# Second weight parts a turn later, six raw buffers, one factor multiply moved and full-row second key parts in a two-layer attention and conv-FFN trunk

## The chip, the cores and the metric

The kernel runs on one core of a Trainium2 chip. The metric is the device time of one execution in microseconds (us); smaller is better. A core has five engines that work side by side, each through its own list of instructions in order: TensorE (PE, matrix products), VectorE (DVE), ScalarE (ACT), GpSimd (POOL) and SyncE (SP, which here issues most DMAs). They wait for each other through semaphores. SBUF is the core's memory with 128 partitions, PSUM the banks into which PE writes.

## What is computed

Two layers over 256 positions of width 1024, in float32. Layer 0 mixes tokens with dilated attention A (three groups of 16 heads of 64, one window and dilation each, merged by their softmax denominators), layer 1 with block attention B. Each layer ends in a gated FFN with a causal convolution of width 3.

```python
for i in range(DEPTH):                       # 2 layers
    hn = rmsnorm(x, attn_norm[i])
    x = x + (mixer_dilated if i % 2 == 0 else mixer_moba)(hn, w_qkv, q_gain, k_gain, w_o, cos, sin)
    hn = rmsnorm(x, ffn_norm[i])
    x = x + conv_ffn(hn, ffn_w_up[i], ffn_conv_w[i], ffn_conv_b[i], ffn_w_down[i])

def mixer_dilated(h, w_qkv, q_gain, k_gain, w_o, cos, sin):
    qkv = (h @ w_qkv).reshape(B, S, 3, N_DIL, N_HEADS, HEAD_DIM)
    q = apply_partial_rope(rmsnorm(qkv[:, :, 0], q_gain[:, None, :]), cos, sin)
    k = apply_partial_rope(rmsnorm(qkv[:, :, 1], k_gain[:, None, :]), cos, sin)
    v = qkv[:, :, 2]
    # per group: scores, mask, softmax, times v; then the groups weighted by denominators
    return attn @ w_o

def conv_ffn(h, w_up, conv_w, conv_b, w_down):
    u = h @ w_up
    uc = conv_b + sum(conv_w[j] * up[:, j:j + S] for j in range(CONV_WIDTH))
    gate, val = uc[..., :D_FF], uc[..., D_FF:]
    return (jax.nn.silu(gate) * val) @ w_down
```

## The kernel before

**Products in two parts.** A float32 product is made of products of rounded numbers: a matrix is split into a first part (`whi` of a weight, a rounded copy) and a second part (`wlo`, the rest), and `mm3` adds three products of 128x512: activations' first part by `whi` (L380), their second part by `whi` (L381), their first part by `wlo` (L382).

**The weight stream.** `Stream` cuts all weights into 244 parts of 128x1024 in the order of use. `load` starts the DMA of a raw part on SP (4 raw buffers, `RAW`); `start` makes `whi` from it on ACT (L85); `finish` makes `wlo` on DVE (L94) and calls `load` again, so the load of a raw part stands behind the `wlo` of the part four before it. `take` hands parts to the products, `release` frees their `whi` and `wlo` (8 of each, `WB`).

**Turns.** All work around the products is placed by `turn`, once for each piece of a product. A turn runs, in this order: `ws.start`, the tasks in the table `first`, one `ws.finish`, the tasks in `pre`, the rest of `ws.finish`, the products themselves (with the tasks in `mid` in them), the tasks in `post`. `at(table, n, task)` puts a task into a table n turns later. Each engine then runs its instructions in the order in which they were written.

**Attention.** For each section of 4 heads, `qk_block` makes q and k. When a block's product is done, ACT copies it (`sq`, `qk`); a turn later `head_sums` runs on DVE (L432 to L444), and POOL makes the factors `rs_y` from it (L257, L259); another turn later `factors` multiplies (L453, DVE); PE transposes (L469), ACT makes the first parts of keys and queries (L505), and `second_parts` makes the rest on DVE (L511, L513). `step_A` makes scores for two heads. For group 0 of attention A the head's own half of the partitions of `qT` and `kT` holds first parts and the other half second or copied first parts, so that L575 contracts all 128 rows; the product with the second parts of the keys, `kL`, contracts the head's 64 rows (L577), for two heads side by side. L590 makes the scores of the other groups from 64x64 pieces. `step_E` takes the masked scores and their maximum on DVE (L603) and the exponentials on ACT (L613); `step_R` scales by the denominator on DVE (L620, L623); `step_T` transposes on PE (L630); `step_V` copies to SBUF (ACT) and `step_C` multiplies by v (L657).

The order within a turn:

```python
        ws.start(min(pump, 1 if len(ws.parts) - ws.taken >= AHEAD else 2))
        for f, a in first.pop(t, ()):
            f(*a)
        ws.finish(1)
        for f, a in pre.pop(t, ()):
            f(*a)
        ws.finish()
```

Of the kernel before, what the change touches and what calls it, by code (L numbers as in the profile page):

```python
# [11 lines left out]
F32R = mybir.dt.float32r  # L12
# [5 lines left out]
P = 128  # L18
# [11 lines left out]
NSEC = NH // HS  # L30
NEG = -1.0e30
PAIRS = ((128, 1), (512, 4), (2048, 16))
RAW, WB, QB, TB, AHEAD = 4, 8, 5, 6, 5

FINE, WARM = 4, 9

PUMPS = (0, 0, 1, 2, 1, 1, 1, 0, 2, 1, 1)

# [8 lines left out]
def r32(ap):  # L47
    return ap.bitcast(F32)


class Stream:
# [33 lines left out]
                    self.nc.scalar.activation(hi[:, i], raw[:, i], AF.Copy)  # L85
                self.parts.append((hi, lo))

    def finish(self, n=WB):

        while self.done < len(self.parts) and n > 0:  # L90
            n -= 1
            hi, lo = self.parts[self.done]
            for i in self.pieces(self.done):
                self.nc.vector.tensor_sub(lo[:, i], self.raw[self.done][:, i], r32(hi[:, i]))  # L94
            self.done += 1
            self.load()
# [5 lines left out]
    def take(self, n):  # L102
        while len(self.parts) < self.taken + n:
            k = len(self.parts)
            self.pump()
            assert len(self.parts) > k
        self.taken += n
        return [(i, *self.parts[i]) for i in range(self.taken - n, self.taken)]

    def release(self, *units):  # L110
# [7 lines left out]
def trunk_kernel(ctx, tc, x, a_w_qkv, a_w_o, b_w_qkv, b_w_o, ffn_norm, ffn_w_up, ffn_w_down, gains, pack, mask_a, mask_b,  # L118
# [61 lines left out]

    def turn(fn, pump=2):
        t = now[0]
        ws.start(min(pump, 1 if len(ws.parts) - ws.taken >= AHEAD else 2))
        for f, a in first.pop(t, ()):
            f(*a)
        ws.finish(1)
        for f, a in pre.pop(t, ()):
            f(*a)
        ws.finish()
        if fn is not None:  # L190
            fn()
        for f, a in post.pop(t, ()):
            f(*a)
        now[0] += 1
# [190 lines left out]
    def attention(xT, norms, ng, g0, mask):  # L385
# [3 lines left out]
        moff = 3 * P if dil else P  # L389
        aT = new_T()  # L390

        def product(done):

            box = {}

            def part(c, u):
                def go():
                    if c == 0:
                        box[u] = ws.take(2)
                    if u == 0:  # L400
                        box["acc", c] = new_acc()
                    for i, (_, hi, lo) in enumerate(box[u]):
                        if i == 1:
                            for f, a in mid.pop(now[0], ()):
                                f(*a)
                        for kk in range(2):
                            k = (u + i) * 2 + kk
                            mm3(box["acc", c], xT, k, c, hi[:, kk].rearrange("p j n -> p (j n)"),
                                lo[:, kk].rearrange("p j n -> p (j n)"), k == 0, k == 7)
                    if c == 1:  # L410
                        ws.release(*box[u])
                    if u == 2:
                        done(c, box["acc", c])
                return go

            for c in range(2):
                for u in (0, 2):
                    yield part(c, u)

        def qk_block(g, res, rq):  # L420
            res.append(None)

            def done(c, acc):
# [6 lines left out]
            def head_sums(c, qk, sq):  # L430
                ssq = sp.tile([P, 8], F32, name="qssq", bufs=2)
                nc.vector.tensor_reduce(ssq, sq.rearrange("p (h d) -> p h d", d=HD), axis=AX.X, op=ALU.add)  # L432
                rs = rsqrt_pool(ssq, 1.0 / HD, norms[c].eps)

                t4 = qk.rearrange("p (j h d) -> p j h d", j=2, d=HD)
                ra = sp.tile([P, 2, HS, 16], F32, name="ra", bufs=1)
                rb = sp.tile([P, 2, HS, 16], F32, name="rb", bufs=1)
                cg = CG[:, c, g0 + g]
                sg = SG[:, c, g0 + g]
                nc.vector.tensor_mul(ra, t4[:, :, :, 0:16], cg[:, :, None, :].to_broadcast([P, 2, HS, 16]))  # L440
                for lo_, hi_ in ((0, 8), (8, 0)):
                    nc.vector.tensor_mul(rb[:, :, :, lo_:lo_ + 8], t4[:, :, :, hi_:hi_ + 8],
                                         sg[:, :, None, lo_:lo_ + 8].to_broadcast([P, 2, HS, 8]))
                nc.vector.tensor_add(t4[:, :, :, 0:16], ra, rb)  # L444
                at(first, 1, factors, c, qk, rs)

            def factors(c, qk, rs):

# [7 lines left out]
            def transpose(c, qk):  # L456
                if c == 0:
                    if dil and g > 0:
                        res[g] = [bp.tile([P, 2, 2, P], F32R, name="t0", bufs=TB) for _ in range(2)]
                    elif dil:  # L460
                        res[g] = [*(bp.tile([P, 2, 2, S], F32R, name="kT", bufs=QB) for _ in range(2)),
                                  bp.tile([P, 2, S], F32R, name="kL", bufs=2)]
                    else:
                        res[g] = (bp.tile([P, 2, 2, P], F32R, name="t0", bufs=TB),
                                  bp.tile([P, 2, 2, P], F32R, name="t0", bufs=TB),
                                  bp.tile([P, 2, 2, S], F32R, name="kT", bufs=QB))
# [18 lines left out]
                if dil and g > 0:  # L485
                    plain(res[g][c])
                elif dil:

                    qT, kT, kL = res[g]
                    for e in range(2):  # L490
                        r, o = slice(e * HD, e * HD + HD), slice(HD - e * HD, P - e * HD)
                        copies.append((kT[r, e, :, cs], k[r], gk[r]))
                        copies.append((qT[r, e, :, cs], q[r], 1.0))
                        subs.append((kT[r, e, :, cs], kL[r, :, cs], k[r], gk[r]))
                        subs.append((qT[r, e, :, cs], qT[o, e, :, cs], q[r], None))
                        at(post, 4 + e, nc.gpsimd.tensor_copy, kT[o, e, :, cs], kT[r, e, :, cs])
                else:
                    t0, q1, kT = res[g]
                    split(kT[:, :, 0, cs], kT[:, :, 1, cs], k, gk)
                    if c == 0:  # L500
                        plain(t0)
                    else:
                        split(q1[:, 0], q1[:, 1], q, None)
# [54 lines left out]
        def step_A(sec, c, heads, qkT, v, rq):  # L558
# [5 lines left out]
            for i in range(0, len(heads), 2):  # L564
# [7 lines left out]
                if dil:  # L572
                    qT, kT, kL = qkT[0]
                    for e, (s2, o, rows, pr) in enumerate(two):
                        nc.tensor.matmul(s2[:, o:o + S], qT[:, e, pr, cs], kT[:, e, pr], start=True, stop=False)  # L575
                    for e, (s2, o, rows, pr) in enumerate(two):
                        nc.tensor.matmul(s2[:, o:o + S], qT[rows, e, pr, cs], kL[rows, pr], start=False, stop=True)  # L577
                else:
                    for a, b in ((0, 0), (1, 0), (0, 1)):
                        for s2, o, rows, pr in two:  # L580
# [89 lines left out]
        for sec in range(NSEC):  # L670
            qk, v, rq = [], vs[sec], {}
            for s, c, heads in last if sec == NSEC - 1 else odd if sec % 2 else plan:
                at(post, s, step_A, sec, c, heads, qk, v, rq)
            gens = [qk_block(g, qk, rq) for g in range(ng)] + ([v_first(v)] if dil else [])
            gens += [v_last(vs[sec // 2 * 2:sec // 2 * 2 + 2])] if sec in V_TURN[ng] else []
            fns = [fn for gen in gens for fn in gen]
            if sec == 0:
# [326 lines left out]
```

## Time and profile before

| what | value |
|---|---|
| median of 3 runs | 798.54 us (798.48 to 799.37) |
| profiled execution: device time | 798.97 us |
| profiled execution: span in the trace | 797.1 us |
| PE busy in the span | 779.1 us, 98% |
| DVE busy | 565.8 us, 71% |
| ACT busy | 487.1 us, 61% |
| POOL busy | 101.3 us, 13% |
| PE's mean granted clock, share of full speed | 0.997 |

The times in the rows below count from the start of the span. By the trace the kernel goes through a start (to about 49 us), the rest of attention A (to 283), its output product (to 304), the first conv-FFN (to 480), attention B (to 590), its output product (to 620) and the second conv-FFN (to 797). A bracket at the end of a row of a timeline is the engine's idle time just before it and what ended it. Ends of matmuls are modelled, so how fast PE goes is read from start to start.

### The profile page before, as it was taken

The page shows a single profiled execution, that of the slowest core. Times are in us where ns is not written, and L with a number is a line of the kernel's source. Part 1 is how long each engine was busy: PE and PEld are TensorE (multiplying, and loading weights), DVE is VectorE, ACT ScalarE, POOL GpSimd, SP SyncE. Part 2 cuts the span into 40 slices and gives each one's busy share as a digit, 9 for nine tenths or more (in the row PEclk, how much of TensorE's full clock was granted, in tenths as well). Part 3 has the DMA queues.
Part 4 walks back from the last instruction along what each step waited for, and adds up shares of the span by engine and source line. Part 5 has one row for each costly group of instructions (what it writes and reads, how often), then busy time and mean ns, then how long its engine had stood idle before and what let it go on. Part 6 is the DMA issues. An engine that isn't in the chain of part 4 may idle for free.

```text
span 797.1 us, 13374 instructions
## 1 busy us (share of the span) xinstructions
PE 779.1 (98%) x5010; PEld 672.5 (84%) x5010; DVE 565.8 (71%) x1026; ACT 487.1 (61%) x827; POOL 101.3 (13%) x133
## 2 busy tenths in 40 slices
PE   8999999999999999999999999999999999999997
PEld 6778878888878779999999988777778999999996
DVE  6885776885686656788667676777757687767762
ACT  7668676676775636556554655867755565555550
POOL 3540241340134000000000002132100000000000
PEclk9999999999999999999999999999999999999999
DMA  8676545445446425566655462743426457655631
GB/s 261 192 236 192 149 128 185 133 153 165 132 138 230 137 80 167 175 212 210 216 186 185 159 206 91 232 133 107 160 79 192 152 175 247 213 159 176 204 124 53
DMA packets 107920, 133.90 MB, mean 168 GB/s; under 512 B 5968, under 2 KB 92368, under 8 KB 107856
## 3 DMA queue, kind: packets, MB, share of 16 engines
q1 hardware_dynamic: 107280, 130.96, 52.3%
q0 software_dynamic: 576, 2.10, 0.7%
q8 instruction: 39, 0.64, 0.4%
q14 instruction: 25, 0.20, 0.1%
HBM read 131.99 MB, written 1.05 MB: 167 GB/s over the span
## 4 chain that ended last, share of the span: by engine, by line
PE 79%; DVE 9%; ACT 4%; POOL 3%; issue 2%; DMA 2%; SPq 0%; DVEq 0%; ACTq 0%; POOLq 0%
PE acc L770 10%; PE acc L769 10%; PE acc L768 10%; PE acc L380 9%; PE acc L382 8%; PE acc L381 8%; DVE wlo L94 3%; PE S L809 3%; PE S L810 3%; PE S L811 3%; PE PT L811 2%; PE PT L809 2%; PE PT L810 2%; PE O L657 2%; PE PT L630 2%
## 5 line engine op out<-in xcount | busy, mean ns | idle before, releaser
L94 DVE TENSOR_TENSOR wlo<-raw,whi 128x1024 fp32r<-128x1024 f32 (+1 forms) x248 | 291.7, 1209 | 80.1 <-ACT whi L85 79.1
L85 ACT ACTIVATE whi<-raw 128x1024 fp32r<-128x1024 f32 (+1 forms) x248 | 249.1, 1039 | 20.6 <-PE PT L810 10.8
L380 PE MATMUL acc<-whi,xT 128*128 128x512 f32 x448 | 183.6, 410 | 2.3 <-ACT whi L85 1.6
L770 PE MATMUL acc<-xT,wlo 128*128 128x256 f32 x640 | 181.1, 283 | 0.0
L768 PE MATMUL acc<-xT,whi 128*128 128x256 f32 x640 | 181.1, 283 | 0.0
L769 PE MATMUL acc<-xT,whi 128*128 128x256 f32 x640 | 181.1, 283 | 0.0
L382 PE MATMUL acc<-wlo,xT 128*128 128x512 f32 x448 | 176.6, 394 | 2.9 <-DVE wlo L94 2.8
L381 PE MATMUL acc<-whi,xT 128*128 128x512 f32 x448 | 175.8, 392 | 0.4 <-DVE xT L369 0.2
L769 PEld LDWEIGHTS acc<-xT,whi 128*128 128x128 f32 x640 | 122.7, 192 | 1.3
L768 PEld LDWEIGHTS acc<-xT,whi 128*128 128x128 f32 x640 | 122.7, 192 | 1.3
L770 PEld LDWEIGHTS acc<-xT,wlo 128*128 128x128 f32 x640 | 122.7, 192 | 0.0
L382 PEld LDWEIGHTS acc<-wlo,xT 128*128 128x128 f32 x448 | 84.4, 188 | 24.0 <-DVE wlo L94 5.4
L380 PEld LDWEIGHTS acc<-whi,xT 128*128 128x128 f32 x448 | 84.5, 189 | 21.9 <-issue 2.6
L381 PEld LDWEIGHTS acc<-whi,xT 128*128 128x128 f32 x448 | 84.7, 189 | 16.9 <-DVE xT L369 1.5
L785 DVE SCALAR_TENSOR_TENSOR qk<-acc,pk,qk 128x255 f32<-128x255 f32 (+1 forms) x160 | 65.9, 473 | 21.4 <-ACT qk L782 21.2
L782 ACT ACTIVATE qk<-acc,pk 128x256 f32<-128x256 f32 x80 | 40.6, 557 | 28.1 <-PE acc L770 28.1
L259 POOL TENSOR_TENSOR rs_y<-rs_v,mhalf 128x8 f32<-128x8 f32 x32 | 53.6, 1674 | 2.7
L794 ACT ACTIVATE kT<-qk 128x512 fp32r<-128x512 f32 x22 | 13.9, 632 | 56.9 <-DVE qk L792 56.9
L257 POOL TENSOR_SCALAR rs_v<-qssq,rn_e 128x8 f32<-128x8 f32 x32 | 14.2, 445 | 216.0 <-DVE qssq L432 215.9
L788 ACT ACTIVATE qk<-qk 128x512 f32<-128x512 f32 x22 | 13.9, 632 | 41.6 <-DVE qk L785 41.6
L809 PE MATMUL S<-whi,kT 128*128 128x512 f32 x88 | 34.7, 394 | 0.0
L810 PE MATMUL S<-whi,kT 128*128 128x512 f32 x88 | 34.7, 394 | 0.0
(130 smaller groups left out, 952.9 us busy)
## 6 DMA issues: line engine op xcount, KB each, us to landing
raw<-in_ffn_w_up_dram SPq DMA_DIRECT2D x80, 512.0 KB, 4.1
raw<-in_a_w_qkv_dram SPq DMA_DIRECT2D x144, 256.0 KB, 4.0
raw<-in_ffn_w_down_dram SPq DMA_DIRECT2D x44, 512.0 KB, 5.0
raw<-in_b_w_qkv_dram SPq DMA_DIRECT2D x48, 256.0 KB, 4.0
raw<-in_a_w_o_dram SPq DMA_DIRECT2D x8, 512.0 KB, 4.1
raw<-in_ffn_w_up_dram SPq DMA_DIRECT2D x16, 256.0 KB, 3.7
raw<-in_b_w_o_dram SPq DMA_DIRECT2D x8, 512.0 KB, 3.9
xr<-in_x_t_dram SPq DMA_DIRECT2D x4, 256.0 KB, 6.1
```

The source lines that it names most:

```text
L85: self.nc.scalar.activation(hi[:, i], raw[:, i], AF.Copy)
L94: self.nc.vector.tensor_sub(lo[:, i], self.raw[self.done][:, i], r32(hi[:, i]))
L259: nc.gpsimd.tensor_tensor(y, v, mhalf[:, 0:n], op=ALU.pow)
L380: nc.tensor.matmul(acc, T[:, k, 0, cs], hi, start=first, stop=False)
L381: nc.tensor.matmul(acc, T[:, k, 1, cs], hi, start=False, stop=False)
L382: nc.tensor.matmul(acc, T[:, k, 0, cs], lo, start=False, stop=last)
L768: nc.tensor.matmul(o, hi[:, k % 4, es], xT[:, k, 0], start=(k == 0), stop=False)
L769: nc.tensor.matmul(o, hi[:, k % 4, es], xT[:, k, 1], start=False, stop=False)
L770: nc.tensor.matmul(o, lo[:, k % 4, es], xT[:, k, 0], start=False, stop=(k == 7))
L785: nc.vector.scalar_tensor_tensor(o[:, d:S], u[:, 0:S - d], cw[:, first_tap + b:first_tap + b + 1], o[:, d:S], op0=ALU.mult, op1=ALU.add)
L809: nc.tensor.matmul(o, acts[f][:, 0, cs], hi[:, sl], start=(b == 0), stop=False)
L810: nc.tensor.matmul(o, acts[f][:, 1, cs], hi[:, sl], start=False, stop=False)
```

## The change

- From turn 12 on (`LATE`) a part started in a turn is finished in the next one: `finish` gets an upper end, the number of parts that there were before the turn's `start`. `take` finishes the parts it hands out.
- The raw parts get six buffers instead of four. To make room, the scratch of POOL's software DMAs is set to 4096.
- In the first section of attention A `factors` is put into the table `pre` instead of `first`.
- `kL` becomes two fixed tiles with a half for each of two heads over all 128 partitions; the half of the partitions that is not the head's own is set to zero once, by four POOL memsets of 64x512. The score product with `kL` contracts all 128 rows, and follows directly on the head's other product.

```diff
-RAW, WB, QB, TB, AHEAD = 4, 8, 5, 6, 5
+RAW, WB, QB, TB, AHEAD = 6, 8, 5, 6, 5
+LATE = 12
...
-    def finish(self, n=WB):
-
-        while self.done < len(self.parts) and n > 0:
+    def finish(self, n=WB, end=None):
+
+        while self.done < (len(self.parts) if end is None else end) and n > 0:
             n -= 1
...
         self.taken += n
+        self.finish(self.taken - self.done)
         return [(i, *self.parts[i]) for i in range(self.taken - n, self.taken)]
...
     def turn(fn, pump=2):
         t = now[0]
+        end = len(ws.parts) if t >= LATE else None
         ws.start(min(pump, 1 if len(ws.parts) - ws.taken >= AHEAD else 2))
         for f, a in first.pop(t, ()):
             f(*a)
-        ws.finish(1)
+        ws.finish(1, end)
         for f, a in pre.pop(t, ()):
             f(*a)
-        ws.finish()
+        ws.finish(end=end)
...
+        kLs = [cp.tile([P, 2, 2, S], F32R, name=f"kL{i}") for i in range(2)] if dil else []
+        for t in kLs:
+            for e in range(2):
+                nc.gpsimd.memset(r32(t[HD - e * HD:P - e * HD, e]), 0.0)
...
-                at(first, 1, factors, c, qk, rs)
+
+                at(pre if dil and sec == 0 else first, 1, factors, c, qk, rs)
...
-                                  bp.tile([P, 2, S], F32R, name="kL", bufs=2)]
+                                  kLs[sec % 2]]
...
-                        subs.append((kT[r, e, :, cs], kL[r, :, cs], k[r], gk[r]))
+                        subs.append((kT[r, e, :, cs], kL[r, e, :, cs], k[r], gk[r]))
...
                         nc.tensor.matmul(s2[:, o:o + S], qT[:, e, pr, cs], kT[:, e, pr], start=True, stop=False)
-                    for e, (s2, o, rows, pr) in enumerate(two):
-                        nc.tensor.matmul(s2[:, o:o + S], qT[rows, e, pr, cs], kL[rows, pr], start=False, stop=True)
+                        nc.tensor.matmul(s2[:, o:o + S], qT[:, e, pr, cs], kL[:, e, pr], start=False, stop=True)
...
-    nc = _bacc.Bacc("TRN2", target_bir_lowering=False, num_devices=1)
+    nc = _bacc.Bacc("TRN2", target_bir_lowering=False, num_devices=1, dynamic_dma_scratch_size=4096)
```

Three places show what this does to the engines' lists. First DVE at the start of attention A, in the first section (`wlo` is the second weight part, `rs_y` the factor from POOL, `qssq` the head sums; L441 to L453, L463 and L96 of the changed kernel are L432 to L444, L453 and L94 of the one before). Before:

```order
L94 TENSOR_TENSOR wlo<-raw,whi 128x1024 x2
L453 TENSOR_TENSOR qk<-qk,rs_y 128x512
L432 TENSOR_REDUCE qssq<-sq 128x8
L440 TENSOR_TENSOR ra<-qk,CG 128x128
L442 TENSOR_TENSOR rb<-qk,SG 128x8x8 x2
L444 TENSOR_TENSOR qk<-ra,rb 128x8x16
L94 TENSOR_TENSOR wlo<-raw,whi 128x1024
```

and after:

```order
L96 TENSOR_TENSOR wlo<-raw,whi 128x1024 x2
L441 TENSOR_REDUCE qssq<-sq 128x8
L449 TENSOR_TENSOR ra<-qk,CG 128x128
L451 TENSOR_TENSOR rb<-qk,SG 128x8x8 x2
L453 TENSOR_TENSOR qk<-ra,rb 128x8x16
L96 TENSOR_TENSOR wlo<-raw,whi 128x1024
L463 TENSOR_TENSOR qk<-qk,rs_y 128x512
```

The multiply by POOL's factor has moved behind the head sums and the next `wlo`.

Second DVE in a softmax step of attention A, the one around 104 us of the trace (`kL`, `kT` with L513 and L511 are second parts of keys and queries, `rd` and `sm` the softmax scaling; the new lines are 523, 521, 629 and 632). Before:

```order
L607 TENSOR_SCALAR nbias<-mx 128x2
L513 SCALAR_TENSOR_TENSOR kL<-acc,gqk,kT 64x2x128
L511 TENSOR_TENSOR kT<-acc,kT 64x2x128
L513 SCALAR_TENSOR_TENSOR kL<-acc,gqk,kT 64x2x128
L511 TENSOR_TENSOR kT<-acc,kT 64x2x128
L94 TENSOR_TENSOR wlo<-raw,whi 128x1024 x2
L620 RECIPROCAL rd<-den 128x2
L623 TENSOR_SCALAR sm<-sm,rd 128x384 x2
L432 TENSOR_REDUCE qssq<-sq 128x8
```

and after:

```order
L616 TENSOR_SCALAR nbias<-mx 128x2
L523 SCALAR_TENSOR_TENSOR kL_176<-acc,gqk,kT 64x2x128
L521 TENSOR_TENSOR kT<-acc,kT 64x2x128
L523 SCALAR_TENSOR_TENSOR kL_176<-acc,gqk,kT 64x2x128
L521 TENSOR_TENSOR kT<-acc,kT 64x2x128
L629 RECIPROCAL rd<-den 128x2
L632 TENSOR_SCALAR sm<-sm,rd 128x384 x2
L441 TENSOR_REDUCE qssq<-sq 128x8
L449 TENSOR_TENSOR ra<-qk,CG 128x128
L451 TENSOR_TENSOR rb<-qk,SG 128x8x8 x2
L453 TENSOR_TENSOR qk<-ra,rb 128x8x16
L96 TENSOR_TENSOR wlo<-raw,whi 128x1024 x2
```

The pair of second weight parts has moved from before the softmax scaling to behind it and the head sums. ACT's list is the same in both kernels.

Third PE in a block of scores (`S` is the bank of scores, `t_502` and the like are the queries and keys of the other groups). Before:

```order
L575 MATMUL S<-kT 128x256 x2
L577 MATMUL S<-kL,kT 128x256 x2
L590 MATMUL S<-t_502 64x64 x2
L590 MATMUL S<-t_648 64x64 x4
L590 MATMUL S<-t_502 64x64 x2
```

and after:

```order
L585 MATMUL S<-kT 128x256
L586 MATMUL S<-kL_175,kT 128x256
L585 MATMUL S<-kT 128x256
L586 MATMUL S<-kL_175,kT 128x256
L599 MATMUL S<-t_513 64x64 x2
L599 MATMUL S<-t_651 64x64 x4
L599 MATMUL S<-t_513 64x64 x2
```

The two heads' products now take turns, and each writes its bank from all 128 rows.

## Rows read from the trace of the kernel before

**Rows 1.** Busy time by stretch: PE, PEld, DVE, ACT, POOL, granted clock, DMA.

```profile
49.00:246.00 197.00, 194.41 (x1252) 158.70 (x1251) 145.43 (x293) 137.94 (x256) 49.14 (x49) 1.00 0.52 158
101.00:109.00 8.00, 6.93 (x36) 5.59 (x36) 7.79 (x20) 7.94 (x17) 0.51 (x1) 1.00 0.23 73
...
304.00:480.00 176.00, 176.00 (x1232) 165.25 (x1231) 126.31 (x176) 98.84 (x135) 1.12 (x4) 1.00 0.61 194
```

**Rows 2.** PE's waits by releaser: us in total, times, longest.

```profile
PE PT L630 <- DVE sm L623: 3.7, 4, 1.1
PE acc L382 <- DVE wlo L94: 2.8, 2, 2.0
...
PE S L581 <- ACT t L505: 1.4, 1, 1.4
...
PE S L569 <- DVE mx L603: 0.7, 1, 0.7
...
PE S L581 <- DVE t L511: 0.5, 1, 0.5
```

**Rows 3.** A costly group of the page: count, busy us, mean ns of one, idle.

```profile
L770 PE MATMUL acc<-xT,wlo 128*128 128x256 f32 x640 | 181.1, 283 | 0.0
```

**Rows 4.** Timeline of DVE at the start of attention A: start, us, instruction.

```profile
25.53 0.69 DVE L453 TENSOR_TENSOR qk<-qk,rs_y 128x512 f32<-128x512 f32 x1 [1.94 <-POOL rs_y L259]
...
27.60 1.22 DVE L94 TENSOR_TENSOR wlo<-raw,whi 128x1024 fp32r<-128x1024 f32 x1
```

**Rows 5.** Timeline of PE there, the two waits for a second part.

```profile
28.88 0.50 PE L382 MATMUL acc<-wlo,xT 128*128 128x512 f32 x1 [1.98 <-DVE wlo L94]
...
40.91 0.50 PE L382 MATMUL acc<-wlo,xT 128*128 128x512 f32 x1 [0.81 <-DVE wlo L94]
```

**Rows 6.** Timeline of POOL, ahead of its tables.

```profile
11.89 1.30 POOL L349 TENSOR_TENSOR qk<-qk 128x512 f32<-128x512 f32 x1 [10.50 <-ACT qk L346]
14.95 0.64 POOL L243 TENSOR_TENSOR CG<-pk 128x96 f32<-128x96 f32 x1 [1.76 <-DMA pk<-in_pack_dram]
```

**Rows 7.** Groups of POOL's instructions by shape: its memsets.

```profile
masks.py:197 POOL MEMSET ident<- 128x128 f32 x1 | 0.2, 205 | 0.3 <-POOLq L990 0.3
...
L216 POOL MEMSET mhalf<- 128x8 f32 x1 | 0.1, 106 | 0.0
```

**Rows 8.** Timelines of PE, DVE and ACT around two softmax steps of attention A.

```profile
92.25 0.60 PE L469 MATMUL acc<-ident,qk 128*128 128x128 f32 x4
92.69 0.82 PE L630 MATMUL PT<-ident,sm 128*128 128x128 f32 x6
...
105.85 0.60 PE L469 MATMUL acc<-ident,qk 128*128 128x128 f32 x4
107.51 0.88 PE L630 MATMUL PT<-ident,sm 128*128 128x128 f32 x6 [1.07 <-DVE sm L623]
...
104.56 2.36 DVE L94 TENSOR_TENSOR wlo<-raw,whi 128x1024 fp32r<-128x1024 f32 x2
106.84 0.16 DVE L620 RECIPROCAL rd<-den 128x2 f32<-128x2 f32 x1
...
105.09 0.19 ACT L613 ACTIVATION_READ_ACCUMULATOR sm<-sm,nbias 128x1 f32 x1
```

**Rows 9.** Timeline of PE in a block of scores of attention A.

```profile
98.81 0.40 PE L575 MATMUL S<-kT 128*128 128x256 f32 x2
99.14 0.38 PE L577 MATMUL S<-kL,kT 64*128 64x256 f32 x2
99.45 0.47 PE L590 MATMUL S<-t 64*64 64x64 f32 x16
```

**Rows 10.** Groups of ACT's instructions from 503 to 508 us, in attention B.

```profile
L85 ACT ACTIVATE whi<-raw 128x1024 fp32r<-128x1024 f32 x3 | 3.2, 1062 | 1.7 <-DMA raw<-in_b_w_qkv_dram 1.7
```

**Rows 11.** Timeline of DVE at an early softmax step.

```profile
61.29 0.17 DVE L620 RECIPROCAL rd<-den 128x2 f32<-128x2 f32 x1 [1.38 <-ACT sm L613]
```

**Rows 12.** Timeline of DVE early in the first conv-FFN.

```profile
321.88 1.65 DVE L785 SCALAR_TENSOR_TENSOR qk<-PT,pk,qk 128x255 f32<-128x255 f32 x4
...
324.95 0.69 DVE L795 TENSOR_TENSOR kT<-qk,kT 128x512 fp32r<-128x512 f32 x1 [0.70 <-ACT kT L794]
```

More of the change, by code (lines that the diff above doesn't have):

```diff
@@ L418, in product, with qk_block @@
                     yield part(c, u)
-        def qk_block(g, res, rq):
+        def qk_block(sec, g, res, rq):
             res.append(None)
@@ L673, in attention @@
                 at(post, s, step_A, sec, c, heads, qk, v, rq)
-            gens = [qk_block(g, qk, rq) for g in range(ng)] + ([v_first(v)] if dil else [])
+            gens = [qk_block(sec, g, qk, rq) for g in range(ng)] + ([v_first(v)] if dil else [])
             gens += [v_last(vs[sec // 2 * 2:sec // 2 * 2 + 2])] if sec in V_TURN[ng] else []
```

## The prediction

> **What bounds the kernel now.** I read first where PE is busy by stretch, then what ends PE's waits, then the timelines of the engine that PE waits for. In the first conv-FFN PE has not a microsecond free: 176.00 of 176.00 us, with VectorE (DVE) at 126 and ScalarE at 99 [rows 1]. Nothing that the change does can shorten that stretch, and it can only lengthen it. In attention A PE is busy 194.41 of 197 us [rows 1]: what is to be had is a few single waits. The view of PE's waits lists them [rows 2]: four times the transposes of the softmax weights (L630) wait for DVE's scaling (L623), 3.7 us; twice a product (L382) waits for a second weight part `wlo`, 2.8 us; once each in attention B, score products wait for L505 on ScalarE (1.4), for L511 on DVE (0.5) and for a free S bank behind L603 (0.7). That is 9.1 us. So the question for each edit is which of these waits it ends, and what stands next in line.
>
> An idle entry understates a wait, since PE also restarts: undisturbed, four L469 are followed by L630 0.44 us later (92.25 to 92.69); at 105.85 it took 1.66 us, with 1.07 us of idle in it [rows 8]. 1.66 - 0.44 - 1.07 = 0.15 us of restart per wait.
>
> **The change, part by part.** The sum is made against the profiled execution, 798.97 us (0.43 above the median of 798.54), as a difference, and then taken off the median.
>
> *The start: head sums before the factor multiply, and zeroing on POOL.* At 25.53 DVE's L453 has waited 1.94 us for POOL's `rs_y`; the head sums and the `wlo` of 27.60 stand behind it, and PE waits 1.98 us for that part until 28.88 [rows 4, 5]. In the new order the head sums and this `wlo` come first. From 25.53 to 27.60 are 2.07 us, of which the multiply is 0.69, so the `wlo` starts at 23.59 + 1.38 = 24.97 and ends at about 26.2, before PE wants it at 28.88 - 1.98 = 26.90. That wait goes. The next one (0.81 us at 40.91) shrinks less than one would think: up to that part DVE has the same instructions in either order, so it comes 1.94 us earlier, at 38.97, but PE, now 1.98 us ahead, wants it at 40.10 - 1.98 = 38.12 and waits 0.85. The gain is 1.98 + 0.81 - 0.85 = 1.94 us, just DVE's own wait.
>
> Against that stand four new POOL memsets of 64x512, which POOL issues between L349 and the tables of L243. POOL runs from 14.95 on with hardly a pause into `rs_y`, so what the memsets push back there, DVE's chain is pushed back too. POOL was idle 1.76 us for a DMA before 14.95 [rows 6]: that is their cover. No memset of this size is in the trace. The two nearest rows are 205 ns for 128x128 and 106 for 128x8 [rows 7]: 99 ns for 120 elements, so 0.106 + 504 x 0.000825 = 0.52 us for 512, 2.09 for four, 0.33 beyond the cover. If width costs nothing more, 4 x 0.205 = 0.82 lies wholly under it; if a memset is as dear as POOL's two-input operation of the same width (1.30, L349), 5.2 us leave 3.44 uncovered. I take the slope, since it is the same operation: 1.94 - 0.33 = **1.6** (from -1.5 to 1.9).
>
> *Second parts a turn later.* At 104.56 two `wlo` (2.36 us) stand on DVE before the softmax step's L620 (106.84); ScalarE's last exponential was done at 105.09 + 0.19 = 105.28, and PE began L630 0.67 us after L620 did [rows 8]. In the new order L620 and L632 (the old L623) follow directly on the second key parts. Then L630 can begin at 105.28 + 0.67 = 105.95; PE is there at 105.85 + 0.44 = 106.29. The wait goes with 0.34 us to spare. The four waits have the same form [rows 2], so 3.7 + 4 x 0.15 = **4.3** (from 0, if the exponential is late each time, to 4.3). The wait for the S bank (0.7, L569 for L603) has one `wlo`, half of that 2.36, in front of DVE's work on the scores; without it DVE is 1.18 earlier: 0.7 + 0.15 = **0.85** (from 0.4, if the `wlo` only partly stood in the way). ScalarE's order is not touched, so what its exponentials wait for is the same.
>
> What is queued behind L620 now waits for the exponential with it: at 61.29 DVE idled 1.38 us there already [rows 11]. And each moved part is late by a turn. In attention that has cover: PE waits for a `wlo` in two places only, both at the start [rows 2, 5]. In the FFNs a moved part falls behind a chain on DVE from 321.88 to 325.64, one L785 group of 1.65 us and a wait for ScalarE in it [rows 12]. PE waits for no `wlo` there now, so at most of the parts the lead covers it; the first ones of each FFN have the shortest lead. I take a loss of **0.15**, from 0 to half a chain, 1.9.
>
> *Full-row second key parts.* A block of scores has two full-row products (L575), two half-row ones (L577) and small ones (L590), starting at 98.81, 99.14 and 99.45: 0.64 us up to L590 [rows 9]. A pair of L575 takes 0.40, a single 128x256 product 0.283 [rows 3, 9], so one follows the other after 0.117, and 99.14 - 98.81 - 0.117 = 0.213 is the passage from full to half rows. The two L577 run side by side, then 0.31 passes to L590. Afterwards four full-row products follow each other: three steps of 0.117, and a last one into L590 which is 0.213 if it costs what the passage to half rows does, 0.31 if L590's form sets it. That is 0.564 or 0.661 for 0.64, in 16 blocks -1.2 or +0.3 us. I take the first, a **gain of 1.2**, since it too leaves full rows for a smaller tile.
>
> The Trainium skill (TensorEngine Tiling (Array Packing), Theoretical Speedup) speaks against this edit: products with at most 64 rows to contract run up to twice as fast as tiles side by side. The rule's count of a pair plus a side-by-side pair is 0.351 us by the 0.117 above; the row has 0.64, and 0.29 of it lies at the passages, so the trace bears out the side-by-side run but not the saving.
>
> *Six raw buffers.* Just before the scores that wait in attention B, ScalarE idles 1.7 us before three `whi`, each time for the DMA of its raw part [rows 10]. A raw part's load is issued when the `wlo` six parts back is done, no longer four. With the two extra parts in flight the loads land before ScalarE asks, and all behind them, L505 among it, comes 1.7 us earlier: more than the 1.4 that PE waits for it. The 0.5 for DVE's L511 goes for the most part, as DVE's `wlo` of that stretch wait for the same `whi`. 1.4 + 0.5 = **1.9** (from 0). The other queue edits, two mask loads that come four and two places elsewhere between the raw loads on SP and a smaller scratch for POOL's own four DMAs, wait for nothing that is late: their price is nothing, and if the x load on POOL came late, the start would show it.
>
> Sum: 1.6 + 4.3 + 0.85 - 0.15 + 1.2 + 1.9 = 9.7 us. 798.97 - 9.7 = 789.3 for a profiled run, and **788.8** on the median's basis.
>
> **Rivals.**
> *POOL's zeroing eats the start.* At L349's price the start loses 1.5 instead of gaining 1.6: 788.8 + 3.1 = 791.9. For it: no row has the price. Against it: a memset reads nothing, and the rows of memsets are a sixth of L349's or less.
> *Six raw buffers bring nothing in B*, because the loads there are late for the queue and not for a buffer: 788.8 + 1.9 = 790.7. For it: the DMA is what ScalarE waited for in all three. Against it: the row's 1.7 us are short waits.
> *Side-by-side products were cheaper.* A pair of half-row products as one step, two full-row ones as two: 0.117 x 16 = 1.9 lost in place of 1.2 gained, 788.8 + 3.1 = 791.9. That is the skill's rule above. Against it stands the 0.29 at the passages.
> *The softmax waits stay*, as waits for the exponential: 788.8 + 4.3 = 793.1. For it: only 0.34 us to spare. Against it: ScalarE has the same order and loses no input.
> *Slower: DVE's in-order queue.* In the dense part of a step DVE is busy 7.79 of 8.00 us [rows 1]; a wait of its own at L620 that nothing fills any more pushes the head sums, the factors and with them PE's transposes back. The 12 steps of the stretch at 1.38 us each [rows 11], less the 0.21 spare, cost 12 x 1.17 = 14.0: 788.8 + 14.0 = 802.8. It decides from (9.7 + 1.6) / 12 + 0.21 = 1.15 us of wait per step. Against it: over the whole stretch DVE has 52 of 197 us free [rows 1], and the wait at 61.29 hurt no one.
>
> **How the numbers follow.** The forecast has a chance of 0.52; POOL 0.13; raw buffers 0.10; side by side 0.06; softmax waits 0.07; slower 0.06. The last 0.06 go to several at once: start, raw buffers and softmax waits together leave 9.7 - 3.1 - 1.9 - 4.3 = 0.4, which is no change. A measurement of this kernel tells about 0.2%, 1.6 us, from no change. So faster 0.88, same 0.06, slower 0.06. The range's lower end is the forecast with the upper ends of its terms (0.3 more at the start, 0.15 in the FFNs) and restarts that I have left out where a wait vanishes between equal products, some 0.15 at a time: 786.5. The upper end takes in each single rival up to 793.1 and a second small miss, 794.5.
>
> **What would show it.** In the profile of the changed kernel: L639 (the old L630) waiting for nothing, or for a scaling that itself follows an exponential at once; one wait of PE for `wlo` near 39 us and none near 27; DVE's idle time moved from "`wlo` for `whi`" to "`rd` for `sm`"; POOL's four memsets and whether the tables still start at 14.95; four score products 0.117 apart and 0.2, not 0.3, before the small ones; no DMA wait of ScalarE before 508. Wrong it is if the FFNs show any wait of PE for `wlo` of more than half a microsecond, or if L639 still waits in most steps.

## The result and the profile after

The changed kernel takes 789.77 us (median of 4 runs, 789.47 to 791.12), against 798.51 us for the kernel before; the ratio is 0.9892 with a 95% interval of 0.9875 to 0.9910. The forecast was 788.8 with a range of 786.5 to 794.5, so 8.7 us were gained where 9.7 were expected. The profiled execution, the fastest of the four, took 789.47 us, with a span of 787.6.

Read first by stretch, as [rows 1] were. Busy time of the changed kernel: PE, PEld, DVE, ACT, POOL, granted clock, DMA:

```profile
49.00:246.00 197.00, 197.00 (x1273) 162.98 (x1272) 147.99 (x301) 140.97 (x260) 50.17 (x53) 1.00 0.51 158
304.00:480.00 176.00, 175.47 (x1220) 164.27 (x1219) 125.11 (x179) 97.91 (x133) 1.11 (x4) 1.00 0.60 189
```

Attention A from 49 us on has no free microsecond on PE any more (194.41 of 197 before). The first conv-FFN, full before, has lost half a microsecond. Then PE's waits, as in [rows 2]:

```profile
PE acc L386 <- DVE wlo L96: 1.7, 2, 1.3
...
PE acc L479 <- DVE qk L463: 0.7, 1, 0.7
PE acc L779 <- DVE wlo L96: 0.5, 1, 0.5
...
PE S L590 <- DVE t L521: 0.2, 1, 0.2
```

L639, the old L630, is gone from the list with its 3.7 us, L579 (the old L569) with its 0.7, and L590 (the old L581) waits 0.2 instead of 1.9. Two entries are new: the transposes L479 wait for a factor multiply, and a product of the conv-FFN (L779) waits for a second part.

PE runs the same 5010 matmuls in both kernels, in the same order but for the score blocks. So the start of one matmul can be compared in the two traces, and where its lead changes is where time was won or lost:

| place | before | after | lead | what changed since the row above |
|---|---|---|---|---|
| second wait for a second part, start | 40.91 | 40.22 | 0.69 | the start: 0.7 |
| first softmax transposes that waited | 107.51 | 105.23 | 2.28 | 1.2 for the wait, 0.4 for score blocks |
| second | 163.57 | 160.33 | 3.24 | 0.7 and 0.3 |
| third | 234.66 | 229.69 | 4.97 | 1.3 and 0.4 |
| conv-FFN, the new wait | 325.92 | 321.10 | 4.82 | -0.75, after 0.6 more from the last score blocks and small waits |
| scores in attention B | 512.81 | 506.61 | 6.20 | 1.4 |
| the S bank | 551.80 | 544.51 | 7.29 | 0.8, and 0.3 at 513.66 |
| fourth softmax transposes | 576.09 | 567.24 | 8.85 | 1.3, after 0.2 more behind the S bank |
| end of the span | 797.1 | 787.6 | 9.5 | small waits at 581 and 589: 0.65 |

**The softmax step.** DVE, ACT and PE around the step of [rows 8]:

```profile
104.26 0.17 DVE L629 RECIPROCAL rd<-den 128x2 f32<-128x2 f32 x1 [0.83 <-ACT sm L622]
104.46 0.75 DVE L632 TENSOR_SCALAR sm<-sm,rd 128x384 f32<-128x384 f32 x2
...
106.52 2.39 DVE L96 TENSOR_TENSOR wlo<-raw,whi 128x1024 fp32r<-128x1024 f32 x2
...
104.04 0.19 ACT L622 ACTIVATION_READ_ACCUMULATOR sm<-sm,nbias 128x1 f32 x1
...
104.80 0.60 PE L479 MATMUL acc<-ident,qk 128*128 128x128 f32 x4
105.23 0.82 PE L639 MATMUL PT<-ident,sm 128*128 128x128 f32 x6
```

The exponential ends at 104.23, L629 follows at once, and L639 begins 0.43 us after L479, as in an undisturbed step. DVE now idles 0.83 us where it used to make second parts, and those come 2.1 us later with nobody waiting.

**A block of scores**, as in [rows 9]:

```profile
97.85 0.28 PE L585 MATMUL S<-kT 128*128 128x256 f32 x1
97.96 0.28 PE L586 MATMUL S<-kL,kT 128*128 128x256 f32 x1
98.08 0.28 PE L585 MATMUL S<-kT 128*128 128x256 f32 x1
98.20 0.28 PE L586 MATMUL S<-kL,kT 128*128 128x256 f32 x1
98.41 0.47 PE L599 MATMUL S<-t 64*64 64x64 f32 x16
```

Three steps of 0.11 to 0.12 and a last one of 0.21: 0.56 us up to L599 where it was 0.64.

**The start.** DVE, POOL and PE; [rows 4 to 6] are the places before:

```profile
25.14 1.22 DVE L96 TENSOR_TENSOR wlo<-raw,whi 128x1024 fp32r<-128x1024 f32 x1
26.28 0.68 DVE L463 TENSOR_TENSOR qk<-qk,rs_y 128x512 f32<-128x512 f32 x1
26.88 1.22 DVE L96 TENSOR_TENSOR wlo<-raw,whi 128x1024 fp32r<-128x1024 f32 x1
29.92 0.69 DVE L463 TENSOR_TENSOR qk<-qk,rs_y 128x512 f32<-128x512 f32 x1 [1.82 <-POOL rs_y L263]
...
12.98 2.21 POOL L399 MEMSET kL<- 64x512 f32 x4
15.16 0.38 POOL L247 TENSOR_TENSOR CG<-pk 128x96 f32<-128x96 f32 x1
...
26.51 1.64 POOL L261 TENSOR_SCALAR rs_v<-qssq,rn_e 128x8 f32<-128x8 f32 x1
28.24 1.65 POOL L263 TENSOR_TENSOR rs_y<-rs_v,mhalf 128x8 f32<-128x8 f32 x1
...
37.78 0.63 PE L479 MATMUL acc<-ident,qk 128*128 128x128 f32 x4 [0.67 <-DVE qk L463]
40.22 0.50 PE L386 MATMUL acc<-wlo,xT 128*128 128x512 f32 x1 [1.34 <-DVE wlo L96]
```

The wait of 1.98 us at 28.88 is gone, and the four memsets take 2.21 us and push POOL's tables from 14.95 to 15.16 in this execution, as good as nothing. But DVE again waits for POOL, 1.82 us at 29.92: the small `rs_v` (L261) took 1.64 us, and PE pays at 37.78 and 40.22.

**The first conv-FFN**, DVE and PE:

```profile
311.87 1.65 DVE L794 SCALAR_TENSOR_TENSOR qk<-acc,pk,qk 128x255 f32<-128x255 f32 x4 [3.70 <-ACT qk L791]
313.44 1.22 DVE L96 TENSOR_TENSOR wlo<-raw,whi 128x1024 fp32r<-128x1024 f32 x1
316.14 1.65 DVE L794 SCALAR_TENSOR_TENSOR qk<-PT,pk,qk 128x255 f32<-128x255 f32 x4 [1.48 <-ACT qk L791]
...
319.22 0.69 DVE L804 TENSOR_TENSOR kT<-qk,kT 128x512 fp32r<-128x512 f32 x1 [0.70 <-ACT kT L803]
319.83 2.35 DVE L96 TENSOR_TENSOR wlo<-raw,whi 128x1024 fp32r<-128x1024 f32 x2
...
321.10 0.38 PE L779 MATMUL acc<-xT,wlo 128*128 128x256 f32 x1 [0.53 <-DVE wlo L96]
```

DVE waits 3.7 us for the first convolution's input with no second part in front of it to fill the time. Then it makes one; the next, which PE is about to need, stands behind the second chain from 316 to 319.8, and PE waits.

### The profile page after: what moved, and what is told of

Read it like the earlier page. It is cut to its first block, busy times and chain, and to the rows that moved or that the text cites. A ratio compares the mean times of both kernels' runs of the same rounds, so it can differ in the third digit from the quotient of the medians.

```text
span 787.6 us, 13318 instructions
## 1 busy us (share of the span) xinstructions
PE 775.9 (99%) x5010; PEld 674.0 (86%) x5010; DVE 561.1 (71%) x1026; ACT 487.5 (62%) x827; POOL 102.4 (13%) x137
## 4 chain that ended last, share of the span: by engine, by line
PE 91%; DVE 4%; ACT 3%; DMA 1%; issue 1%; SPq 0%; DVEq 0%; ACTq 0%
PE acc L384 12%; PE acc L386 12%; PE acc L385 12%; PE acc L779 9%; PE acc L778 9%; PE acc L777 9%; PE S L818 3%; PE S L819 3%; PE S L820 3%; PE PT L818 2%; PE PT L820 2%; PE PT L819 2%; PE O L666 2%; PE PT L639 2%; PE acc L479 2%; DVE wlo L96 1%
## 5 line engine op out<-in xcount | busy, mean ns | idle before, releaser
L96 DVE TENSOR_TENSOR wlo<-raw,whi 128x1024 fp32r<-128x1024 f32 (+1 forms) x248 | 290.0, 1206 | 17.8 <-ACT whi L87 17.6
L779 PE MATMUL acc<-xT,wlo 128*128 128x256 f32 x640 | 181.2, 283 | 0.5 <-DVE wlo L96 0.5
L779 PEld LDWEIGHTS acc<-xT,wlo 128*128 128x128 f32 x640 | 122.7, 192 | 0.7 <-DVE wlo L96 0.7
L261 POOL TENSOR_SCALAR rs_v<-qssq,rn_e 128x8 f32<-128x8 f32 x32 | 15.4, 480 | 206.7 <-DVE qssq L441 206.5
```

The costliest lines, as they stand in the source:

```text
L779: nc.tensor.matmul(o, lo[:, k % 4, es], xT[:, k, 0], start=False, stop=(k == 7))
```

## The experiments

Three questions were open: which edit brings what, why POOL's small instruction was so long, and whether the two losses can be had back. Ratios are to the kernel before on the same chip, whose median there was 798.95, 799.53 and 799.70 us in the three groups of runs. The changed kernel's 789.77 us is not from these groups, so beside one of their medians the ratios are the fairer comparison.

### One edit at a time

*The deferral alone*, with four raw buffers, as in the diff ahead:

```diff
+LATE = 12
...
-        ws.finish(1)
+        ws.finish(1, end)
...
-        ws.finish()
+        ws.finish(end=end)
```

> The kernel before with the deferral of second weight parts alone (four raw buffers stay). Theory: the softmax waits go by themselves, as in the changed kernel: PE's four waits of L630 for L623 (4.8 us from start to start) and the wait for the S bank at 551.80 (0.9), and the conv-FFN's new wait for a second part near 321 costs 0.8. That gives 798.5 - 4.9 = 793.6. Rival: with four raw buffers a second part made a turn later sends the next load a turn later, ScalarE waits for DMA and PE for first parts: then the gain is under 2 us, or the time rises, and ScalarE's idle time for DMA in attention A grows by several us. Second rival: the softmax waits turn into waits for the exponential: 797 or more.

Measured: 798.64 us, ratio 0.9990 (0.9980 to 1.0000): next to nothing. The theory and the first rival came true at once, though the DMA waits did not grow in attention A, where the rival had put them (3.0 us against 3.7). In the trace the four softmax waits are gone (L633, the old L630, stands in no list of PE's waits), but ScalarE waits for the DMA of raw parts, 55 us over all matrices against 5.9 before, and PE for ScalarE. ScalarE's waits, then ScalarE and PE in attention B, then the granted clock behind that wait:

```profile
ACT whi L86 <- DMA raw<-in_ffn_w_up_dram: 38.5, 20, 2.9
...
ACT whi L86 <- DMA raw<-in_b_w_qkv_dram: 7.4, 4, 3.8
...
505.78 1.06 ACT L86 ACTIVATE whi<-raw 128x1024 fp32r<-128x1024 f32 x1 [1.72 <-DMA raw<-in_b_w_qkv_dram]
508.39 1.06 ACT L86 ACTIVATE whi<-raw 128x1024 fp32r<-128x1024 f32 x1 [1.55 <-DMA raw<-in_b_w_qkv_dram]
...
514.04 0.58 PE L584 MATMUL S<-kT,t 64*128 64x256 f32 x2 [3.01 <-ACT t L508]
...
514.00:518.00 4.00, 3.69 (x14) 0.50 0.19 60
```

A load stands behind the second part four before it. That part now comes a turn later, and so does the load. In the FFN most of the 38.5 us are covered, though the part there also came later and PE waited 1.1 us for it; in attention B the wait doubles, from 1.4 to 3.0 us. By the comparison of starts with the kernel before, this execution gains 6.5 us at the softmax steps, the S bank and the small waits behind them, and loses 7.4: 1.4 in the conv-FFN, 1.0 at 480 us (a wait for VectorE), 1.6 at the scores in attention B, 2.5 by the lower clock behind them, and 0.9 at the start, where the clock fell too. So a good part of the gain was lost to the clock; all ten runs of this kernel had a mean clock of 0.991 to 0.997.

*Six raw buffers alone*:

```diff
-RAW, WB, QB, TB, AHEAD = 4, 8, 5, 6, 5
+RAW, WB, QB, TB, AHEAD = 6, 8, 5, 6, 5
-    nc = _bacc.Bacc("TRN2", target_bir_lowering=False, num_devices=1)
+    nc = _bacc.Bacc("TRN2", target_bir_lowering=False, num_devices=1, dynamic_dma_scratch_size=4096)
```

> The kernel before with six raw buffers (and the smaller scratch) alone. Theory: only the wait of the scores near 512.8 in attention B goes, 1.8 us from start to start: 796.7, with no DMA wait of ScalarE between 503 and 508 us. Rival: the loads there are late for the queue and not for a buffer: 798.5, and the waits stay. Second rival: that wait went in the changed kernel because second parts came later, not because of the buffers: 798.5 too, but with ScalarE's DMA waits gone.

Measured: 797.81 us, ratio 0.9982 (0.9972 to 0.9991). PE at the scores in attention B:

```profile
512.65 0.38 PE L581 MATMUL S<-kT,t 64*128 64x256 f32 x2
513.51 0.50 PE L581 MATMUL S<-kT,t 64*128 64x256 f32 x4 [0.47 <-DVE t L511]
```

The first wait is gone, the second stays: buffers cure the DMA wait and no more, 1.4 us in the trace instead of 1.8. ScalarE's waits for raw parts are 0.6 us in all. The smaller scratch, which this kernel has too, is not the cure: the full-row kernel below has it with four buffers, and there ScalarE still waits 4.6 us for raw parts, and PE 1.0 at these scores.

*The factor multiply alone*:

```diff
-                at(first, 1, factors, c, qk, rs)
+                at(pre if dil and sec == 0 else first, 1, factors, c, qk, rs)
```

> The kernel before with the factor multiply of the first section behind a split, alone. Theory: POOL's rs_v (L257) beside a second weight part on DVE takes 1.1 to 1.6 us instead of 0.35 to 0.5; the new order puts a second part beside the second chunk's rs_v, so it takes about 1.6 here too, without any memset, and the gain at the start is 0.9 and not 1.9: 797.6. Rival: the memsets of the changed kernel were what delayed POOL there: then rs_v takes 0.35, the second multiply starts near 28.5 and the gain is 1.9: 796.6. In either case PE waits near 37.8 for the third multiply only if that comes late.

Measured: 799.15 us, ratio 1.0002 (0.9989 to 1.0015), so not even 0.9 showed in the median. POOL, then PE, then the granted clock:

```profile
25.84 1.64 POOL L257 TENSOR_SCALAR rs_v<-qssq,rn_e 128x8 f32<-128x8 f32 x1
...
39.55 0.75 PE L382 MATMUL acc<-wlo,xT 128*128 128x512 f32 x1 [1.34 <-DVE wlo L94]
...
41.37 0.63 PE L380 MATMUL acc<-whi,xT 128*128 128x512 f32 x1
41.79 0.63 PE L381 MATMUL acc<-whi,xT 128*128 128x512 f32 x1
...
40.00:42.00 2.00, 2.00 (x6) 0.50 0.67 207
```

There is no memset in this kernel, and `rs_v` still takes 1.64 us: the rival that blamed the memsets falls. By the comparison of starts the edit gained 0.6 us up to that wait (the theory said 0.9). In this execution the lower clock behind the wait of 39.55 then cost 1.6 us, and another 1.6 behind the waits at 513 us (see the last section).

*The full-row second key parts alone*: tiles, memsets and products as in the diff ahead, with the smaller scratch:

```diff
-                        nc.tensor.matmul(s2[:, o:o + S], qT[rows, e, pr, cs], kL[rows, pr], start=False, stop=True)
+                        nc.tensor.matmul(s2[:, o:o + S], qT[:, e, pr, cs], kL[:, e, pr], start=False, stop=True)
```

> The kernel before with the full-row second key parts alone (memsets, fixed tiles, interleaved products). Theory: each of 16 blocks is 0.09 us shorter from its first product to L590, 1.4 us in all, and four memsets of 0.55 us push POOL's first factor back by 0.2 to 0.4, which PE pays in full at 28.88 in this order: 797.3. Rival: side-by-side products were cheaper: 0.117 x 16 = 1.9 more, 800.4. Second rival: the memsets cost the start 1 us or more, and the time is that of before.

Measured: 797.88 us, ratio 0.9992 (0.9982 to 1.0002). The interval does not tell 1.1 us from none, but the blocks in the trace do:

```profile
100.39 0.28 PE L580 MATMUL S<-kT 128*128 128x256 f32 x1
...
100.95 0.47 PE L594 MATMUL S<-t 64*64 64x64 f32 x16
```

0.56 us as in the changed kernel. Side by side was not cheaper.

The medians of the four alone differ by -0.3, -1.1, +0.2 and -1.1 us from the kernel before, 2.3 in sum. Together they gained 8.7. So at least two of them need each other.

### The deferral with six buffers

> The deferral together with six raw buffers, the start and the score products as before. Theory: deferral alone lost its gain to ScalarE's DMA waits (55 us in place of 5.9), since the loads stand behind the second parts; with six buffers these waits are near nothing, so the two together keep all of the softmax waits (5.8) and of the wait in attention B (1.8) less the conv-FFN's 0.8: 798.5 - 6.9 = 791.6. Rival: the parts just add: 0 and 0.9, so 797.6, and the rest of the changed kernel's gain came from the start or the score products.

Measured: 791.31 us, ratio 0.9899 (0.9884 to 0.9914), that is 8.2 us less than before on that chip and 7.5 in the trace. This settles it: ScalarE's list of waits has no raw part left, and the softmax waits stay gone. The deferral takes PE's waits away, the buffers pay for it.

*Five buffers*, in the changed kernel (`RAW = 5`):

> The changed kernel with five raw buffers in place of six. Theory: a part deferred by a turn keeps its raw buffer about a part longer, and up to two parts are open at a time; with four buffers ScalarE waited 55 us for DMA, with six not at all. With five one of the two extra buffers is missing, so ScalarE's waits for DMA lie between, some 5 to 25 us, mostly in the conv-FFNs where they are covered, and attention B keeps part of its wait: 790.5 to 793. Rival: the deferral needs just one buffer more: no waits, 789.8. Second rival: it needs both, and the time is near that of four buffers, 796 or more.

Measured: 790.32 us, ratio 0.9874 (0.9845 to 0.9902), not to be told from six by the time. In the trace ScalarE waits for a raw part once, and PE at the scores for ScalarE:

```profile
ACT whi L87 <- DMA raw<-in_b_w_qkv_dram: 0.9, 1, 0.9
...
PE S L590 <- ACT t L515: 0.4, 1, 0.4
```

My 5 to 25 us were far too many: one buffer more removes almost all of the waits, and the second one removes the last, worth some 0.7 us at 508 us.

### Why POOL's small instruction was long

In the trace of before the first `rs_v` already took more than others of its kind, and DVE made a second part at the time:

```profile
22.61 1.12 POOL L257 TENSOR_SCALAR rs_v<-qssq,rn_e 128x8 f32<-128x8 f32 x1
...
22.38 1.22 DVE L94 TENSOR_TENSOR wlo<-raw,whi 128x1024 fp32r<-128x1024 f32 x1
```

It ends at 23.73, the second part at 23.60. In the changed kernel the second `rs_v` ends at 28.15 and the second part beside it (26.88 and 1.22) at 28.10. All other `rs_v` of this size in both traces, with only short DVE instructions beside them, take 0.34 to 0.51 us. The test puts POOL's instructions in another order: both `rs_v` first, then both `rs_y`.

```diff
-        nc.gpsimd.tensor_tensor(y, v, mhalf[:, 0:n], op=ALU.pow)
+        held.append((y, v, n))
+        if not hold:
+            for y_, v_, n_ in held:
+                nc.gpsimd.tensor_tensor(y_, v_, mhalf[:, 0:n_], op=ALU.pow)
+            held.clear()
...
-                rs = rsqrt_pool(ssq, 1.0 / HD, norms[c].eps)
+                rs = rsqrt_pool(ssq, 1.0 / HD, norms[c].eps, hold=dil and sec == 0 and g + c == 0)
```

> The changed kernel with POOL's instructions at the start in another order: both chunks' rs_v ahead of both rs_y, so that the second rs_v runs near 24.7 us, beside short instructions of DVE, and not beside a second weight part. Theory (a two-input second part on DVE holds POOL up until it ends): this rs_v takes 0.35 to 0.5 us and not 1.64, the second rs_y ends near 28.6 and not 29.89, DVE's chain and with it PE's second part come 1.2 us earlier than 40.22, and the third multiply no longer keeps PE waiting at 37.78: 789.8 - 1.2 = 788.6. Rival: the long rs_v has another cause (its place behind rn_e, or the first use of something): it stays over 1 us, and the time is 789.8 or, since the first multiply is later, 790.5.

Measured: 787.98 us, ratio 0.9857 (0.9844 to 0.9871). POOL, then PE:

```profile
24.88 0.35 POOL L263 TENSOR_SCALAR rs_v<-qssq,rn_e 128x8 f32<-128x8 f32 x1 [0.36 <-DVE qssq L447]
25.31 3.42 POOL L268 TENSOR_TENSOR rs_y<-rs_v,mhalf 128x8 f32<-128x8 f32 x2
...
39.17 0.50 PE L392 MATMUL acc<-wlo,xT 128*128 128x512 f32 x1 [0.80 <-DVE wlo L96]
```

The second `rs_v` takes 0.35 us, both factors are there at 28.73, the transposes no longer wait, and PE's second part comes at 39.17. By the comparison of starts PE gains 1.4 us there, and the median is 1.8 lower than that of the changed kernel (as ratios, 0.9857 against 0.9892). The theory holds.

### The conv-FFN

Second parts are made in the same turn again in the conv-FFNs (a flag that `attention` sets and `ffn` clears):

```diff
-        end = len(ws.parts) if t >= LATE else None
+        end = len(ws.parts) if t >= LATE and late[0] else None
```

> The changed kernel with second parts made in the same turn again in the conv-FFNs, deferred only in attention and the output products. Theory: the wait of PE for a second part at 321 us (0.8 from start to start) goes and nothing else changes: 789.0. Rival: the raw buffers are then freed earlier or later than is good for attention B and its wait comes back: 790 or more.

Measured: 790.55 us, ratio 0.9889 (0.9873 to 0.9905), runs from 788.45 to 792.16. The trace is that of the 788.45. DVE in front of the same chain:

```profile
313.18 1.22 DVE L96 TENSOR_TENSOR wlo<-raw,whi 128x1024 fp32r<-128x1024 f32 x1
```

The part that PE needs near 320 is ready at 314.40, PE waits for no second part of the FFN, and the comparison of starts shows 0.8 us gained at that place. The median doesn't show it: four of the five runs had a mean granted clock of 0.997 and 790.25 to 792.16 us. Where the clock fell in them no trace tells, so that the loss lies at the start, where this kernel still has the wait of 1.3 us, is only likely.

*Both mends together*:

> The two together, POOL's order at the start and second parts without deferral in the conv-FFNs. If both theories hold, the two add, as they lie in different stages: 789.8 - 1.2 - 0.8 = 787.8. If only one holds, 788.6 or 789.0.

Measured: 787.60 us, ratio 0.9852 (0.9839 to 0.9866), runs from 787.45 to 787.78. It beats both kernels, 2.2 us under the changed one's median (0.9852 against 0.9892); against POOL's order alone it is 0.4 lower in the median, which the intervals do not tell from none, and 1.0 in the span (785.6 against 786.6). Of this 1.0 the starts put 0.6 at the conv-FFN; the other 0.4 was there before 27 us, where the two kernels do not differ.

## Why the prediction was right, point by point

**Softmax waits and the S bank: right.** Forecast 4.3 + 0.85; the starts show 1.2 + 0.7 + 1.3 + 1.3 = 4.5 and 0.8. The margin of 0.34 us held: the exponential was in time in each of the four. Taking the restart from two rows, and not only the idle time, made the difference between 3.7 and 4.3, and still was a little short.

**Attention B: right in size, and for the first wait by the mechanism named.** Forecast 1.9; 1.7 in the starts, and six buffers alone gave 1.4 of it. The second wait, for DVE's L511, was to go with the buffers too. With six buffers alone it stayed at 0.47; it shrank to 0.2 where the second parts were deferred as well.

**Score blocks: right.** Forecast 1.2; 0.64 to 0.56 us in 16 blocks is 1.3 (the starts show 0.07 to 0.09 a block). The choice between the two exits, 0.213 or 0.31, was the right one: L586 to L599 takes 0.21. The Trainium skill's rule on side-by-side tiles (TensorEngine Tiling (Array Packing), Theoretical Speedup) would have made the blocks longer; the measurement decides against it here.

**The price of the memsets: right.** 2.09 us for four was worked out from two rows, 2.21 measured; 0.2 instead of 0.33 stuck out. The second number is that of one execution: in the six traces with memsets POOL's tables start between 14.73 and 16.18 us, as L349 ahead of them comes earlier or later.

**The start: the term was mis-sized.** Forecast 1.6, measured 0.7. The step that failed is "up to that part DVE has the same instructions in either order, so it comes 1.94 us earlier". The instructions are the same, but what POOL does beside them is not. The new order fills DVE's wait with a second part, and that second part stops POOL's `rs_v`, on which DVE's next multiply hangs: 1.64 - 0.35 = 1.3 us, which is what POOL's new order gave back (1.4). Two rows of the trace of before showed it, 22.61 on POOL and 22.38 on DVE, and I read past them since they were not on the chain that I followed.

**The conv-FFN: the term was mis-sized.** Forecast 0.15, measured 0.75. The mechanism, a part behind the chain of 321.88 [rows 12], was the right one. But "at most of the parts the lead covers it" was a guess for the first parts, where the chain is longest: DVE also waits there for ScalarE within it (3.7 us in front of 311.87, 1.48 and 0.70 behind it). The prediction named its own sign of being wrong here, a wait of PE for `wlo` of more than half a microsecond in an FFN: the 0.53 us at 321.10 is one, if by little.

**How the edits hang together: not foreseen.** The prediction booked 5 us on the deferral and 1.9 on the buffers and did not say that one needs the other. The deferral alone is worth nothing and the buffers alone 1.1; together 8.2. The rule for it was in the prediction, that a load stands behind the second part six, or four, before it; what was not asked is what that does to loads when the second parts come a turn later.

**The sum: close, and in part by luck.** The start and the conv-FFN together fell 1.5 us short of their terms. Small waits that had no term made up about 1 us of it in the trace, 0.65 at 581 and 589 us alone, and so the spans differ by 9.5 us where 9.7 was forecast. The medians differ by 8.7.

Of the rivals none came: the zeroing was cheap, side-by-side products were not cheaper, the DMA waits went with the buffers, no softmax wait came back as a wait for the exponential, and DVE's own waits there hurt nobody: at L629 in the twelve steps of that stretch of attention A they are 8.1 us in all against 7.3 before, 0.7 a step (0.83 at 104.26, 1.38 at most), under the 1.15 a step from which they would have decided.

## What to carry to other kernels

Where two edits touch one ring of buffers, cost them together: moving a consumer later lengthens the hold on its buffer, and the loads behind it pay unless the ring grows, here 55 us of DMA waits with four buffers and none with six. When a wait on one engine is to be filled with other work, look at what that work does to the engine that is being waited for; a row that is three times as long as its like is worth a question before the change is made. And apply a deferral only in the stages in which the deferred work stands in somebody's way: in the conv-FFN nothing waited, and there it could only lose, 0.75 us in the trace (the medians don't show it).

## What the runs showed of the hardware

**DVE's second parts hold POOL up; POOL holds them up much less.** `rs_v`, a POOL instruction on 128x8 that takes 0.34 to 0.51 us, ended each time with the second part beside it (1.12 us in the traces of before and after, 1.64 in that of after and again with the multiply alone). In the kernel with both mends the first `rs_v` had two second parts beside it, one right behind the other, and it took 2.15 us, to the end of the second:

```profile
21.59 2.15 POOL L264 TENSOR_SCALAR rs_v<-qssq,rn_e 128x8 f32<-128x8 f32 x1
...
21.33 2.36 DVE L96 TENSOR_TENSOR wlo<-raw,whi 128x1024 fp32r<-128x1024 f32 x2
```

The Trainium skill (SBUF — State Buffer, the section on SBUF's two separate sides) says that DVE and POOL share a pair of ports, held by one for a whole instruction, and that a DVE instruction with two SBUF inputs is among those that hold it against a POOL instruction that reads SBUF. The traces agree for `rs_v` beside `wlo`. They show less for the reverse: in the kernel with POOL's new order a `wlo` runs from 27.75 for 1.21 us, no longer than the median of 1.22, while POOL is in `rs_y` until 28.73. Beside POOL's casts of 64x256, though, a second part takes 1.41 or 1.42 us, 0.2 more, four times in the trace of the changed kernel, for example:

```profile
108.19 1.78 POOL L197 CAST kT<-kT 64x256 fp32r<-64x256 f32 x2
...
109.63 1.42 DVE L96 TENSOR_TENSOR wlo<-raw,whi 128x1024 fp32r<-128x1024 f32 x1
```

**A long wait of PE can cost twice.** After PE had waited 0.88 and 1.34 us close together (factor multiply alone), 3.01 us (deferral alone) or some 2 us at 29 us (deferral, six buffers and full rows, each alone), the granted clock fell in the profiled execution to 0.50, that is 1.2 GHz, for about 3 us, and for about 6 us behind the 3.01: products of 128x512 then follow each other every 0.43 us and not every 0.23, some 1.5 us more, or 2.5. In the traces of before and of the deferral with six buffers it did not happen behind the same wait at 29 us, nor in that of after behind 0.67 and 1.34 us, so it is not certain each time. In the ten runs of the factor multiply alone the four with a mean clock of 1.000 took 797.1 to 798.2 us, the four with 0.995 took 800.1 to 801.4. The kernel with both mends, in which PE waits nowhere longer than 1.0 us once its first transposes have begun, spreads over 0.3 us. That this spread is narrow because no long wait is left is not shown: no run changed the length of one wait alone, and the deferral with six buffers, which keeps a wait of 2.0 us, spreads over 0.7 us only.
